# Six edits to the order, buffers and engines of a tuned two-block kernel on one core: group products given their own priority, a norm's short chain on GpSimd, a new pool for a residual

## Chip, cores and metric

One core of a Trainium2 chip. The metric is the device time of one execution in microseconds (us), the median of several runs; lower is better. Engines are written as in the profile: PE (TensorE matmuls), PEld (its weight loads), DVE (VectorE), ACT (ScalarE), POOL (GpSimd), SP (SyncE, which here only issues loads).

## The reference, cut to what matters

Two blocks in a row on 512 positions of width 1024, all in float32. The first mixes 8 heads of causal attention with 4 heads of a gated recurrence, adds a cross attention over 256 memory rows and a squared-ReLU feed-forward. The second holds a conv branch, a state-space branch (SSD) and a gated feed-forward. The lines the change touches:

```
x1  = x + concat([fox, rec]) @ w_out                  # output product of the mixer
kv  = rmsnorm(mem) @ w_xkv                            # memory keys, the very first product
x2  = rmsnorm(x1 + cross(x1) + ff(...), final_norm_g) # end of block one
hn  = rmsnorm(x2, mix_pre_g)                          # start of block two, right behind it
# SSD, 8 groups of 4 heads, chunks of 64 in the reference (128 in the kernel):
cb     = einsum("bclgn,bcsgn->bgcls", c_mat, b_mat)
y_diag = einsum("bgcls,bgrcls,bcsgrp->bclgrp", cb, decay_in, xdt)
y_off  = einsum("bclgn,bcgrpn,bgrcl->bclgrp", c_mat, prev, exp(a_cs))
y      = y_diag + y_off + x * d_skip
```

## The kernel before

Activations lie transposed, channels on the partitions and the 512 positions along the free axis, in 8 tiles of 128x512. A float32 product is made of three passes of a faster format: a value is split into a high part (`wh`, `xh`, cast on ACT) and a remainder (`wl`, `xl`, subtracted on DVE), and `mm3` (L148) adds hi·hi, hi·lo and lo·hi into one `acc` tile. `gemm_tile` (L154) makes one 128x512 tile of output from one 512 KB block of weights: 8 row blocks times 3 passes, 24 matmuls. Below, such a matmul (L150, L151 or L152) is called a product. The loads of weight blocks go through SP, their split through ACT (L138) and DVE (L139), and all 343 of these carry a priority of 300, so that they run ahead.

The engines' instruction lists are written by a scheduler from the program's order and from priorities. `tc.high_priority(n)` gives what stands inside it places counted from n ahead of where the program has it (a negative n: behind), and after the block the count goes on from where the block began; so a block and what follows it compete for the same places. `keep_in_program_order` pins an instruction to its place among others that are pinned. The scheduler decides the order once; on the chip each engine runs its list in that order, so whatever stands behind a waiting instruction waits too.

A norm over channels works thus: ACT squares each tile (L214), DVE adds the squares into `sqa` (L215), PE sums over partitions with a column of ones (`col_sum`, L223, 4 small matmuls), DVE scales (L229), POOL takes the power -0.5 (L231, `rsqrt_col`), PE spreads the result over the partitions (`row_bc`, L238, 4 matmuls) and ACT copies it out as a tile `R`.

Places the change touches, in the order of time:

- **The first blocks.** The memory keys, 8 blocks of 256-column products; block 0 is made by hand at L283, blocks 1 to 7 by `gemm_tile` at L291.
- **The output product** (L589). For each of 8 tiles the residual `xr` is loaded from `xT` into a tile of the pool `nrm` with the tag "sq", of which there are two. The squares of every norm use the same two.
- **The cross attention's** `nm` column (L637), 4 buffers of 8 bytes.
- **The end of block one** (L700 to L718). Two column sums are taken, of the squares (for `r1`) and of the squares times the gain (for `r2`). Both go through `rsqrt_col`, with three small DVE products between, and PE's L238 spreads `r2` as the tile `R`.
- **The SSD groups** (L983 on). For each g of 8, `group_a(g)` makes transposes (L861, L868), `cb` (L878), states (L886) and the products that give y (L916). Then `group_in(g+1)` makes four whole weight blocks with a short conv, then follow `glu`, `z_in`, gates and `group_b(g)`.

The matmuls of L916 are unlike the others. Each writes 64 output partitions (half r of two, by `r * 64`), so its weights are 128x64 and the profile gives its form as 128*64, where the products have 128*128. 14 of them make one half e of a group (8 with `mt` and `xd`, 6 with `Ct` and `st`): 2 x 8 x 14 = 224. In the trace each is two records, since its operands are plain float32. They are pinned to their order among themselves.

Of the kernel before, what the change touches and what calls it, by code (L numbers as in the profile page):

```python
# [6 lines left out]
F32 = mybir.dt.float32  # L7
# [4 lines left out]
ALU = mybir.AluOpType  # L12
# [22 lines left out]
LATE = 30  # L35
LATE2 = 15
LATE3 = 100
X0 = 0
X1 = 0
X2 = 30  # L40
X3 = 40
# [27 lines left out]
def _build(tc, nc, es, a, out):  # L69
# [79 lines left out]
    def mm3(ps, lh, ll, rh, rl, start, stop):  # L149
        T.matmul(out=ps, lhsT=lh, rhs=rh, start=start, stop=False)  # L150
        T.matmul(out=ps, lhsT=lh, rhs=rl, start=False, stop=False)  # L151
        T.matmul(out=ps, lhsT=ll, rhs=rh, start=False, stop=stop)  # L152

    def gemm_tile(src_blocks, xs, n=S):  # L154

# [110 lines left out]
    with es_mx:  # L266
        ms_ = []
        ac = nrm.tile([P, S], F32, tag="sqa", name="sqa")
        raw = raw0
        hi = whip.tile([P, 8, P], F32R, tag="wh", name="wh")  # L270
        lo = wlop.tile([P, 8, P], F32R, tag="wl", name="wl")
        nc.sync.dma_start(out=vec[:, 8:], in_=a["vec"][:, 8:])
        with tc.high_priority(2000):
            for k in range(0, 8, 2):
                c = slice(k, k + 2)
                G.tensor_copy(out=hi[:, c, :], in_=raw[:, c, :])
                V.tensor_tensor(out=lo[:, c, :], in0=raw[:, c, :], in1=hi[:, c, :].bitcast(F32), op=ALU.subtract)
                for kk in (k, k + 1):
                    ms_.append(split_act(mt[kk], vcol("norm_mem_g", kk), pl=pmx, n=M, tag="m"))
        ps0 = acc.tile([P, S], F32, tag="acc", name="acc")  # L280
        for k in range(8):
            mm3(ps0[:, :M], hi[:, k, :], lo[:, k, :], *ms_[k], k == 0, k == 7)
            if k in (1, 3, 5):  # L283

                for _ in range(FILL):
                    tc.keep_in_program_order(T.matmul(out=wps[:, 0:P], lhsT=ones, rhs=ones, start=True, stop=True))
        for n in range(8):
            if n == 2:
                for k in range(8):
                    nc.sync.dma_start(out=h[k], in_=a["xT"][k * P:(k + 1) * P, :])  # L290
            ps = gemm_tile([(a["w_xk"][n], 8)], ms_, M) if n else ps0  # L291
            A.copy(out=mk[n // 2][:, n % 2, :], in_=ps[:, :M])
        with tc.high_priority(400):
            for k in range(8):
                sq_acc(ac[:, :M], k, mt[k])
        Rm = pm.tile([P, M], F32, tag="Rm", name="Rm", bufs=1)
        with tc.high_priority(400):
            rm = rsqrt_col(col_sum(ac, 2), 2, D)
        with tc.high_priority(-X3):
            A.copy(out=Rm, in_=row_bc(rm, 2))  # L300
        ax = nrm.tile([P, S], F32, tag="sqa", name="sqa")
        for k in range(8):
            sq_acc(ax, k, h[k])
        for n in range(8):
            V.tensor_tensor(out=mk[n // 2][:, n % 2, :], in0=mk[n // 2][:, n % 2, :], in1=Rm, op=ALU.mult)
        R, rc = norm_fin(ax, D, 4, pl=pmx, late=X3)
        xs = []
        for k in range(8):
            V.scalar_tensor_tensor(out=h[k], in0=h[k], scalar=vcol("norm_mix_g", k), in1=R, op0=ALU.mult, op1=ALU.mult)
            xs.append(split_act(h[k]))  # L310
        for hf in range(2):
            def cb(j, ps):
                for i in range(2):
                    A.activation(out=mv[2 * hf + i][:, j, :], in_=ps[:, i * M:(i + 1) * M], func=AF.Copy,
                                 scale=rm[:, j:j + 1])
            gemm_tok(a["w_xv"][hf], ms_, 2, cb)


    with ExitStack() as ea:
# [264 lines left out]
        for i in range(4):  # L584
            g_gg(i)
        eh.close()
        ys = [split_act(mix[k]) for k in (4, 5, 6, 7, 0, 1, 2, 3)]
        h = []
        for n in range(8):  # L589
            xr = nrm.tile([P, S], F32, tag="sq", name="xr")  # L590
            nc.scalar.dma_start(out=xr, in_=a["xT"][n * P:(n + 1) * P, :])
            ps = gemm_tile([(a["w_out"][n], 8)], ys)
            t = hres.tile([P, S], F32, tag=f"h{n}", name=f"h1_{n}")
            V.tensor_tensor(out=t, in0=xr, in1=ps, op=ALU.add)  # L594
            h.append(t)
# [11 lines left out]
    with ExitStack() as ec:  # L607
# [19 lines left out]
        def cross_head(hd, q):  # L627
            PTh = pc.tile([P, 2, S], F32R, tag="PTh", name="PTh", bufs=1)
            PTl = pc.tile([P, 2, S], F32R, tag="PTl", name="PTl", bufs=1)
            for j in range(4):  # L630
                sl = slice(j * P, (j + 1) * P)
                ps = mA()
                mkh, mkl = mks[hd]
                for kk in range(2):
                    qh, ql = q[kk]
                    mm3(ps[:, :M], qh[:, sl], ql[:, sl], mkh[:, kk, :], mkl[:, kk, :], kk == 0, kk == 1)
                nm = pc.tile([P, 2], F32, tag="nm", name="nm", bufs=4)  # L637
                V.tensor_reduce(out=nm[:, 0:1], in_=ps[:, :M], axis=AX.X, op=ALU.max, negate=True)
                Pm = pc.tile([P, M], F32, tag="Pm", name="Pm", bufs=3)
                A.activation(out=Pm, in_=ps[:, :M], func=AF.Exp, bias=nm[:, 0:1], accum_out=nm[:, 1:2])  # L640
                V.reciprocal(out=nm[:, 1:2], in_=nm[:, 1:2])
                V.tensor_scalar(out=Pm, in0=Pm, scalar1=nm[:, 1:2], scalar2=None, op0=ALU.mult)
                pt = mB()
                for i in range(2):
                    T.transpose(out=pt[:, i * P:(i + 1) * P], in_=Pm[:, i * P:(i + 1) * P], identity=ident)
                pt = pt[:, :M].rearrange("p (i c) -> p i c", c=P)
                A.copy(out=PTh[:, :, sl], in_=pt)
                V.tensor_tensor(out=PTl[:, :, sl], in0=pt, in1=PTh[:, :, sl].bitcast(F32), op=ALU.subtract)
# [58 lines left out]
        sq_acc(ac2, k, h[k], vcol("final_norm_g", k))  # L707
    r1 = ctile([P, 4], F32, "r1")
    with tc.high_priority(-LATE2):
        V.tensor_copy(out=r1, in_=rsqrt_col(col_sum(ac1, 4), 4, D))  # L710
        v2 = nrm.tile([P, 4], F32, tag="rv2", name="rv2", bufs=1)
        V.tensor_tensor(out=v2, in0=col_sum(ac2, 4), in1=r1, op=ALU.mult)
        V.tensor_tensor(out=v2, in0=v2, in1=r1, op=ALU.mult)
        r2 = rsqrt_col(v2, 4, D)
        V.tensor_tensor(out=r2, in0=r2, in1=r1, op=ALU.mult)
    R = pre.tile([P, S], F32, tag="R12", name="R12")
    with tc.high_priority(-2 * LATE2):
        A.copy(out=R, in_=row_bc(r2, 4))  # L718
# [211 lines left out]
    def group_b(g, ys, zs):  # L930
# [4 lines left out]
            sq_acc(ac, e, zs[e])  # L935
        with tc.high_priority(-APRI):
            r = rsqrt_col(col_sum(ac, 4, mC), 4, 256)
        with tc.high_priority(-BPRI):
            Rg = row_bc(r, 4, mC)
            res = []  # L940
            for e in range(2):
                V.scalar_tensor_tensor(out=zs[e], in0=zs[e], scalar=vcol("ssm_norm_g_2", 2 * g + e), in1=Rg, op0=ALU.mult,
                                       op1=ALU.mult)
                res.append(split_act(zs[e]))
# [36 lines left out]
    cur = group_in(0, early)  # L981
    gq = list(range(8, 16)) + list(range(8))
    for g in range(8):  # L983
        ys = group_a(g, *cur)
        bg(BG[1])
        if g < 7:
            cur = group_in(g + 1)
# [252 lines left out]
```

## Time and profile before

| what | value |
|---|---|
| median of 3 runs | 1916.11 us (1915.81 to 1916.19) |
| the profiled execution: its time, its span | 1916.54 us, 1914.8 us |
| mean granted clock of PE | 0.997 of full speed |
| busy share of the span: PE, PEld, DVE, ACT, POOL | 99%, 82%, 63%, 45%, 5% |

The span is the time from the first to the last instruction; 1.74 us of the execution lie around it. Matmuls overlap in the pipeline of PE, so a record of 0.39 us doesn't mean that products come 0.39 us apart. The time of a place on PE is read from the starts of neighbouring records, and that is how the numbers below are made. What stands in brackets behind a row is idle time of that engine just before, and what ended it.

### The profile page before, as it was taken

How to read it: one execution, taken by the hardware profiler on the slowest of the kernel's cores; microseconds unless marked ns; L12 is line 12 of the kernel's file. 1: busy time of each engine (PE TensorE's matmuls, PEld its weight loads, DVE VectorE, ACT ScalarE, POOL GpSimd, SP SyncE). 2: the span in 40 equal slices, each digit the busy share in tenths (PEclk: the TensorE clock that was granted, in tenths of full speed). 3: DMA queues.
4: the chain of work that ended last, by engine and by line, in shares of the span. 5: the costliest groups of instructions: out<-in, count | busy, mean ns of one | idle time of the engine just before them, and what ended most of it. 6: DMA issues, size and time to landing. Idle time of an engine off the chain costs nothing.

```text
span 1914.8 us, 25080 instructions
## 1 busy us (share of the span) xinstructions
PE 1892.4 (99%) x9680; PEld 1573.7 (82%) x9680; DVE 1207.1 (63%) x1886; ACT 861.7 (45%) x1393; POOL 101.8 (5%) x198
## 2 busy tenths in 40 slices
PE   9999999999999999999999999999999999999997
PEld 8887776877888888877888888888888988888897
DVE  6744756655443344467888989578997774324456
ACT  6524547444331233348545553545344653222344
POOL 1001110000000000011110110110000000000000
PEclk9999999999999999999999999999999999999999
DMA  7412212322323333344333333333345532233244
GB/s 259 132 57 86 67 54 80 100 66 78 94 95 98 99 99 104 110 95 142 119 122 108 108 119 105 107 115 103 102 141 186 165 91 98 83 116 98 90 130 145
DMA packets 67542, 208.84 MB, mean 109 GB/s; under 512 B 8536, under 2 KB 15448, under 8 KB 67424
## 3 DMA queue, kind: packets, MB, share of 16 engines
q1 hardware_dynamic: 57856, 184.09, 30.9%
q0 software_dynamic: 5968, 16.87, 3.0%
q10 hardware_dynamic: 3600, 6.30, 0.9%
q8 instruction: 76, 1.25, 0.3%
q14 instruction: 42, 0.34, 0.1%
HBM read 198.71 MB, written 8.54 MB: 108 GB/s over the span
## 4 chain that ended last, share of the span: by engine, by line
PE 51%; issue 2%; DVE 1%; DMA 1%; ACT 0%; POOL 0%; POOLq 0%; DVEq 0%; ACTq 0%
PE acc L150 16%; PE acc L151 16%; PE acc L152 16%; PE pb L916 1%; PE pa L886 1%; PE pc L238 0%; PE pa L878 0%; PE pa L868 0%; PE pc L223 0%; PE pa L238 0%; DMA ab<-acsd 0%; DMA wr<-w_dn 0%; PE pa L223 0%; POOL rc L231 0%; PE pa L861 0%
## 5 line engine op out<-in xcount | busy, mean ns | idle before, releaser
L138 ACT CAST wh<-wr 128x1024 fp32r<-128x1024 f32 (+1 forms) x343 | 347.1, 1013 | 714.7 <-PE acc L151 585.1
L139 DVE TENSOR_TENSOR wl<-wr,wh 128x1024 fp32r<-128x1024 f32 (+1 forms) x343 | 403.2, 1176 | 287.4 <-ACT wh L138 277.8
L150 PE MATMUL acc<-yh,wh 128*128 128x512 f32 (+1 forms) x1112 | 432.9, 390 | 0.1
L152 PE MATMUL acc<-yh,wl 128*128 128x512 f32 (+1 forms) x1112 | 431.2, 388 | 0.0
L151 PE MATMUL acc<-yl,wh 128*128 128x512 f32 (+1 forms) x1112 | 429.8, 387 | 0.0
L152 PE MATMUL acc<-xh,wl 128*128 128x512 f32 (+1 forms) x832 | 313.7, 377 | 0.3 <-DVE wl L139 0.3
L150 PE MATMUL acc<-xh,wh 128*128 128x512 f32 (+1 forms) x832 | 313.7, 378 | 0.3 <-DVE h L594 0.3
L151 PE MATMUL acc<-xl,wh 128*128 128x512 f32 (+1 forms) x832 | 313.1, 377 | 0.0
L150 PEld LDWEIGHTS acc<-yh,wh 128*128 128x128 f32 x1112 | 209.1, 188 | 42.0 <-issue 1.4
L152 PEld LDWEIGHTS acc<-yh,wl 128*128 128x128 f32 x1112 | 209.1, 188 | 40.9
L151 PEld LDWEIGHTS acc<-yl,wh 128*128 128x128 f32 x1112 | 209.1, 188 | 40.3 <-DVE yl L202 0.4
L150 PE MATMUL acc<-uh,wh 128*128 128x512 f32 (+1 forms) x520 | 183.9, 354 | 0.0
L151 PE MATMUL acc<-ul,wh 128*128 128x512 f32 (+1 forms) x520 | 183.7, 353 | 0.0
L152 PE MATMUL acc<-uh,wl 128*128 128x512 f32 (+1 forms) x520 | 183.6, 353 | 0.0
L807 DVE SCALAR_TENSOR_TENSOR cv<-gp,vec,cv 128x512 f32<-128x512 f32 x240 | 177.6, 748 | 6.0 <-ACT cv L805 3.0
L150 PEld LDWEIGHTS acc<-xh,wh 128*128 128x128 f32 x832 | 157.1, 189 | 29.3 <-issue 1.5
L152 PEld LDWEIGHTS acc<-xh,wl 128*128 128x128 f32 x832 | 157.2, 189 | 28.7 <-issue 1.8
L151 PEld LDWEIGHTS acc<-xl,wh 128*128 128x128 f32 x832 | 157.2, 189 | 27.0 <-issue 1.2
L152 PEld LDWEIGHTS acc<-uh,wl 128*128 128x128 f32 x520 | 98.3, 189 | 13.5
L150 PEld LDWEIGHTS acc<-uh,wh 128*128 128x128 f32 x520 | 98.3, 189 | 13.4
L151 PEld LDWEIGHTS acc<-ul,wh 128*128 128x128 f32 x520 | 98.4, 189 | 13.3
L231 POOL TENSOR_TENSOR rc<-rv,mhalf 128x4 f32<-128x4 f32 (+1 forms) x25 | 29.7, 1188 | 966.4 <-DVE rv L229 883.2
(364 smaller groups left out, 2111.8 us busy)
## 6 DMA issues: line engine op xcount, KB each, us to landing
wr<-w SPq DMA_DIRECT2D x64, 512.0 KB, 3.8
wr<-w_gu SPq DMA_DIRECT2D x44, 512.0 KB, 3.5
wr<-w_out SPq DMA_DIRECT2D x24, 512.0 KB, 3.5
wr<-w_dn SPq DMA_DIRECT2D x24, 512.0 KB, 3.6
wr<-w_xs SPq DMA_DIRECT2D x16, 512.0 KB, 3.5
wr<-w_glu SPq DMA_DIRECT2D x16, 512.0 KB, 3.5
ab<-acsd POOLq DMA_DIRECT2D x32, 256.0 KB, 3.6
wr<-w_z SPq DMA_DIRECT2D x16, 512.0 KB, 3.5
```

What stands on the lines that cost most here:

```text
L138: A.copy(out=hi[:, :n], in_=raw[:, :n])
L139: V.tensor_tensor(out=lo[:, :n], in0=raw[:, :n], in1=hi[:, :n].bitcast(F32), op=ALU.subtract)
L150: T.matmul(out=ps, lhsT=lh, rhs=rh, start=start, stop=False)
L151: T.matmul(out=ps, lhsT=lh, rhs=rl, start=False, stop=False)
L152: T.matmul(out=ps, lhsT=ll, rhs=rh, start=False, stop=stop)
L231: G.tensor_tensor(out=r[:, :nt], in0=v[:, :nt], in1=mhalf[:, :nt], op=ALU.pow)
L807: yield V.scalar_tensor_tensor(out=o, in0=gp[:, t:t + S], scalar=cw(t), in1=o, op0=ALU.mult, op1=ALU.add)
L886: T.matmul(out=ps[:, 0:256], lhsT=Bt[:, c, :], rhs=xw[:, c].rearrange("p r d -> p (r d)"), start=True, stop=True)
L916: m = T.matmul(out=dst[r * 64:r * 64 + 64, c * P:(c + 1) * P], lhsT=lh, rhs=rh, start=True, stop=True)
```

## The change

1. Block 0 of the memory keys is made by pairs of row blocks, with hi·mh, lo·mh and hi·ml for each pair. Block 1 is made by a new function `gemm_lo_last`: all 16 products with `wh`, then the 8 with `wl`.
2. `xr` has a pool of its own, `pxr`, with two buffers.
3. `nm` has 8 buffers instead of 4, which moves the rest of its pool from an offset of 32 bytes to one of 64.
4. At the end of block one `v1` and `v2` are scaled on DVE, and the rest of the chain for `r1` and `r2` (two powers, three products, one addition on 128x4) is on POOL.
5. `group_a` stands in `tc.high_priority(-40)` for group 0 and in `tc.high_priority(0)` for groups 1 to 7. For group 7 the spread of the norm in `group_b` is set 24 further back.
6. `X0` goes from 0 to 10; it is the offset of one norm in the tail.

```diff
+G0 = 40
-X0 = 0
+X0 = 10
+    def gemm_lo_last(src, xs, n):
+        ps = acc.tile([P, S], F32, tag="acc", name="acc")
+        wh, wl = wblock(src, 8)
+        for w, e in ((wh, 0), (wh, 1), (wl, 0)):
+            for k in range(8):
+                T.matmul(out=ps[:, :n], lhsT=w[:, k, :], rhs=xs[k][e], start=w is wh and e + k == 0, stop=w is wl and k == 7)
+        return ps
...
-        for k in range(8):
-            mm3(ps0[:, :M], hi[:, k, :], lo[:, k, :], *ms_[k], k == 0, k == 7)
-            if k in (1, 3, 5):
+        for k in range(0, 8, 2):
+            for i, (w, e) in enumerate(((hi, 0), (lo, 0), (hi, 1))):
+                for kk in (k, k + 1):
+                    T.matmul(out=ps0[:, :M], lhsT=w[:, kk, :], rhs=ms_[kk][e], start=i + kk == 0, stop=i + kk == 9)
+            if k < 6:
...
-            ps = gemm_tile([(a["w_xk"][n], 8)], ms_, M) if n else ps0
+            ps = ps0 if n == 0 else gemm_lo_last(a["w_xk"][n], ms_, M) if n == 1 else gemm_tile([(a["w_xk"][n], 8)], ms_, M)
...
+        pxr = ea.enter_context(pool("pxr", 2, reuse_waits="tile"))
-            xr = nrm.tile([P, S], F32, tag="sq", name="xr")
+            xr = pxr.tile([P, S], F32, tag="xr", name="xr")
...
-                nm = pc.tile([P, 2], F32, tag="nm", name="nm", bufs=4)
+                nm = pc.tile([P, 2], F32, tag="nm", name="nm", bufs=8)
...
-        V.tensor_copy(out=r1, in_=rsqrt_col(col_sum(ac1, 4), 4, D))
+        v1 = nrm.tile([P, 4], F32, tag="rv", name="v1")
+        V.tensor_scalar(out=v1, in0=col_sum(ac1, 4), scalar1=1.0 / D, scalar2=EPS, op0=ALU.mult, op1=ALU.add)
-        V.tensor_tensor(out=v2, in0=col_sum(ac2, 4), in1=r1, op=ALU.mult)
-        V.tensor_tensor(out=v2, in0=v2, in1=r1, op=ALU.mult)
-        r2 = rsqrt_col(v2, 4, D)
-        V.tensor_tensor(out=r2, in0=r2, in1=r1, op=ALU.mult)
+        V.tensor_scalar(out=v2, in0=col_sum(ac2, 4), scalar1=1.0 / D, scalar2=None, op0=ALU.mult)
+        G.tensor_tensor(out=r1, in0=v1, in1=mhalf, op=ALU.pow)
+        G.tensor_tensor(out=v2, in0=v2, in1=r1, op=ALU.mult)
+        G.tensor_tensor(out=v2, in0=v2, in1=r1, op=ALU.mult)
+        G.tensor_scalar(out=v2, in0=v2, scalar1=EPS, scalar2=None, op0=ALU.add)
+        r2 = nrm.tile([P, 4], F32, tag="rc", name="r2", bufs=4)
+        G.tensor_tensor(out=r2, in0=v2, in1=mhalf, op=ALU.pow)
+        G.tensor_tensor(out=r2, in0=r2, in1=r1, op=ALU.mult)
...
-        with tc.high_priority(-BPRI):
+        with tc.high_priority(-BPRI if g < 7 else -BPRI - 24):
...
-        ys = group_a(g, *cur)
+        with tc.high_priority(-G0 if g == 0 else 0):
+            ys = group_a(g, *cur)
```

What this does to the instruction lists is shown at three places. The first is PE's list in group 1, first half. L916 is the line of the column-tiled matmuls, L936 after the change; L150 to L152 (L151 to L153 after) are the products of the weight block that is running. Before:

```order
L150 MATMUL acc<-yh,wh 128x512
L151 MATMUL acc<-yl,wh 128x512
L152 MATMUL acc<-yh,wl 128x512
L916 MATMUL pb<-mt,xd 64x128 [waits DVE_49]
L916 MATMUL pb<-mt,xd 64x128 x7
L916 MATMUL pb<-Ct,st 64x128 x2
L916 MATMUL pb<-Ct,st 64x128 [waits DVE_49]
```

And now:

```order
L153 MATMUL acc<-yh,wl 128x512
L936 MATMUL pb<-mt,xd 64x128 [waits DVE_49]
L151 MATMUL acc<-yh,wh 128x512
L936 MATMUL pb<-mt,xd 64x128
L152 MATMUL acc<-yl,wh 128x512
L936 MATMUL pb<-mt,xd 64x128
L153 MATMUL acc<-yh,wl 128x512
L936 MATMUL pb<-mt,xd 64x128
```

The 14 stood in one piece between two products; now one product stands between each two of them. Over all groups the 224 stood in 17 pieces (15 of 14, one of 12, one of 2) and now stand in 111: 8 of 14, two of 5, one of 2 and 100 single ones. The second half of a group stays in one piece in groups 0 to 6.

The second place is ACT's list ahead of the first group, from the second half of the first score tile `ab` to the SiLU of `Bt` (L785 before, L805 after), which PE's first transpose of the group (L861 before, L881 after) reads. Before:

```order
L905 ACTIVATE ab<-ab,acc__6612 128x128 [waits DMASW4_49]
L906 ACTIVATE mt<-ab 128x512 [waits Activation_49]
L785 ACT_TABLE_LOAD
L785 ACTIVATE xt<-xt 128x512 [waits DVE_49]
L138 CAST wh<-wr 128x1024 [waits DMAHW5_49,PE_49]
L785 ACTIVATE xt<-xt 128x512 [waits DVE_49]
L905 ACTIVATE ab<-ab,acc__6612 128x128
L785 ACTIVATE Bt<-Bt 128x512 [waits DVE_49]
```

And now:

```order
L139 CAST wh<-wr 128x1024 [waits DMAHW4_49,PE_49]
L805 ACT_TABLE_LOAD
L805 ACTIVATE xt<-xt 128x512 [waits DVE_49] x2
L798 COPY xp<-acc 128x512 [waits PE_49]
L801 ACTIVATE xt<-acc,vec 128x512 [waits DMASW1_49,DMASW0_49]
L925 ACTIVATE ab<-ab,acc__6614 128x128
L925 ACTIVATE ab<-ab,acc__6614 128x128 [waits DMASW4_49]
L926 ACT_TABLE_LOAD
L926 ACTIVATE mt<-ab 128x512 [waits Activation_49]
L139 CAST wh<-wr 128x1024 [waits DMAHW5_49,PE_49]
L805 ACT_TABLE_LOAD
L805 ACTIVATE Bt<-Bt 128x512 [waits DVE_49]
```

Ahead of `Bt` stand two more loads of a function table, one more cast of weights (the one with DMAHW4 stood ahead of all of this before), one more copy `xp` and one more activation of `xt`. PE's first transpose that reads it stands 7 products later than before.

The third place is PE's list at the norm behind the output product; L223 (L233) sums the squares, L238 (L248) spreads the result. Before:

```order
L223 MATMUL pc<-ones,sqa 128x1 [waits DVE_49]
L223 MATMUL pc<-ones,sqa 128x1 x3
L150 MATMUL acc<-xh,wh 128x512
L151 MATMUL acc<-xl,wh 128x512
L238 MATMUL pc<-ident,rc 128x128 [waits Pool_49]
L238 MATMUL pc<-ident,rc 128x128 x3
```

And now:

```order
L233 MATMUL pc<-ones,sqa 128x1 [waits DVE_49]
L233 MATMUL pc<-ones,sqa 128x1 x3
L151 MATMUL acc<-xh,wh 128x512
L152 MATMUL acc<-xl,wh 128x512
...
L152 MATMUL acc<-xl,wh 128x512
L248 MATMUL pc<-ident,rc 128x128 [waits Pool_49]
L153 MATMUL acc<-xh,wl 128x512
L248 MATMUL pc<-ident,rc 128x128
```

Two products stood between the sum and the spread, now 17, and the sum stands some 20 products further ahead.

Two more places, in words. At the end of block one 13 products stood between the second column sum (L223) and the spread of `r2` (L238); now 4 do. In the part of the tail that `X0` sets, the lists of all engines are the same as before.

## Rows read from the trace of the kernel before

**Rows 1.** The page, busy time, share of the span and count by engine.

```profile
PE 1892.4 (99%) x9680; PEld 1573.7 (82%) x9680; DVE 1207.1 (63%) x1886; ACT 861.7 (45%) x1393; POOL 101.8 (5%) x198
```

**Rows 2.** Timeline of PE, group 1, first half: start, us, line, form, count.

```profile
930.17 0.40 PE L152 MATMUL acc<-yh,wl 128*128 128x512 f32 x1
930.50 1.09 PE L916 MATMUL pb<-mt,xd 128*64 128x128 f32 x16
931.42 0.83 PE L916 MATMUL pb<-Ct,st 128*64 128x128 f32 x12
932.18 0.50 PE L150 MATMUL acc<-yh,wh 128*128 128x512 f32 x1
932.51 0.39 PE L151 MATMUL acc<-yl,wh 128*128 128x512 f32 x1
```

**Rows 3.** Timeline of PE, group 0, where two matmuls of L916 stand alone.

```profile
883.23 0.39 PE L150 MATMUL acc<-yh,wh 128*128 128x512 f32 x1
883.55 0.44 PE L916 MATMUL pb<-Ct,st 128*64 128x128 f32 x4
883.92 0.50 PE L151 MATMUL acc<-yl,wh 128*128 128x512 f32 x1
884.25 0.39 PE L152 MATMUL acc<-yh,wl 128*128 128x512 f32 x1
884.49 0.39 PE L150 MATMUL acc<-yh,wh 128*128 128x512 f32 x1
```

**Rows 4.** A tenth of that stretch, L916 alone: records under way.

```profile
core 0: us, PE busy (x) PEld busy (x), PEclk, DMA share, GB/s
883.50:883.60 0.10, 0.05 (x2) 0.05 (x2) 1.00 0.00 0
```

**Rows 5.** Timeline of PE, first block, where matmuls of another small form alternate with products.

```profile
80.55 0.50 PE L150 MATMUL acc<-xh,wh 128*128 128x512 f32 x1
80.99 0.22 PE L347 MATMUL pc<-ident,Fr 8*128 8x8 f32 x1
81.14 0.50 PE L151 MATMUL acc<-xl,wh 128*128 128x512 f32 x1
```

**Rows 6.** Timeline of PE, ahead of group 0.

```profile
872.41 0.39 PE L151 MATMUL acc<-yl,wh 128*128 128x512 f32 x1
874.25 0.55 PE L861 MATMUL pa<-ident,Bt 128*128 128x128 f32 x3 [1.45 <-ACT Bt L785]
```

**Rows 7.** Timeline of ACT, ahead of group 0.

```profile
869.99 1.28 ACT L785 ACT_TABLE_LOAD   x1
...
871.82 1.03 ACT L138 CAST wh<-wr 128x1024 fp32r<-128x1024 f32 x1
...
873.58 0.61 ACT L785 ACTIVATE Bt<-Bt 128x512 f32<-128x512 f32 x1
```

**Rows 8.** Timeline of PE, the first blocks.

```profile
12.95 0.39 PE L152 MATMUL acc<-mh,wl 128*128 128x256 f32 x1 [0.90 <-DVE wl L139]
...
18.09 0.61 PE L223 MATMUL pa<-ones,sqa 128*128 128x1 f32 x4 [0.20 <-DVE sqa L215]
```

**Rows 9.** Timeline of DVE, the same stretch.

```profile
17.09 0.95 DVE L215 TENSOR_TENSOR sqa<-sqa,sq 128x256 f32<-128x256 f32 x2
```

**Rows 10.** Timeline of PE, end of block one.

```profile
836.62 1.13 PE L238 MATMUL pa<-ident,rc 128*128 128x128 f32 x8 [0.88 <-DVE rc L715]
```

**Rows 11.** Timeline of POOL, the second power there.

```profile
835.27 1.01 POOL L231 TENSOR_TENSOR rc<-rv,mhalf 128x4 f32<-128x4 f32 x1 [2.56 <-DVE rv L229]
```

**Rows 12.** Groups of POOL by line and form: count, busy us, mean ns of one.

```profile
L508 POOL TENSOR_TENSOR nD<-nF,cmask 128x128 f32<-128x128 f32 x32 | 15.6, 491 | 76.0 <-DVE Sx L513 71.2 <-DMA nF<-nFd 3.6 <-DVE nm L518 1.0
...
L777 POOL MEMSET xp<- 128x3 f32 x28 | 2.8, 105 | 211.5 <-DMA gated<-gt 132.5 <-DVE xt L784 61.5 <-DVE gp L798 17.4
```

**Rows 13.** Timeline of PE, the norm behind the output product.

```profile
365.27 1.05 PE L223 MATMUL pc<-ones,sqa 128*128 128x1 f32 x8 [0.31 <-DVE sqa L215]
...
367.68 1.87 PE L238 MATMUL pc<-ident,rc 128*128 128x128 f32 x8 [0.78 <-POOL rc L231]
```

**Rows 14.** The stretch behind it: busy by engine (count), granted clock.

```profile
369.00:371.20 2.20, 2.20 (x8) 1.81 (x8) 1.13 (x1) 0.58 (x1) 0.00 (x0) 0.50 0.00 0
```

## The prediction

> **What bounds the kernel now.** The first look goes to the page's busy time: PE is at work for 1892.4 of 1914.8 us, and no other engine comes near [rows 1]. So PE's list sets the end almost everywhere. An edit gains only where PE stands idle or takes long for something, and costs wherever it makes PE's own list slower. The second look is the timeline of PE, read by the starts of records. A product comes 0.23 us behind the one before (884.25 to 884.49) [rows 3]. Whatever exceeds 0.23 per product is an idle stretch or the price of what stands between. The third look is at the places where PE idles, by the releaser in the brackets. The waits that the change aims at are small: 0.90 and 0.20 in the first blocks [rows 8], 0.31 and 0.78 behind the output product [rows 13], 0.88 at the end of block one [rows 10] and 1.45 ahead of group 0 [rows 6]. That is 4.5 us in all.
>
> The rows that decide are others: what PE loses where it goes from a product on the whole array to a matmul on part of it, and back.
>
> **The priority of the groups.** In groups 1 to 7 the matmuls of L916 now alternate with products. Their price is read from the trace.
>
> A run of 14: from 930.17, the last product ahead, to 932.51, the second behind, are 2.34 us [rows 2]. Two products account for 0.46, so the run costs 1.88.
>
> A run of two: from 883.23 to 884.25 are 1.02 us [rows 3]; less 0.46 this is 0.56.
>
> Twelve more matmuls cost 1.32, which is 0.11 each or 0.22 a pair. So of a run's price 0.34 is paid once, for going in and out, whatever its length.
>
> A single L916 isn't in the trace. Bounds: a matmul of 8 columns that alternates with products has a period of 81.14 − 80.55 = 0.59, so it costs 0.36 [rows 5]. It does far less work, so that is the floor. The ceiling is the pair, 0.56. Which is nearer depends on whether the two of a pair run beside one another, in the two halves of the array. In the first tenth of a microsecond of the lone pair two records are under way [rows 4], and the four records of the pair follow from 883.55 on, with 883.92 the next product [rows 3]. Two that start together means that a single one saves nothing by being alone: it leaves half of the array empty for as long as the pair would fill it. I take 0.56. If they ran one behind the other, it would be 0.56 − 0.11 = 0.45.
>
> Before: 15 runs x 1.88 + 0.34 + 6 x 0.22 for the run of 12 + 0.56 = 30.4. After: 8 x 1.88 + 100 x 0.56 + 0.56 + two runs of 5 at about 1.0 = 73.6. The term is **+43.2**; with singles at 0.45 +32, at 0.36 +23. Other matmuls of a group also stand alone between products now, but their form is 128*128, the products' own, and they pay no such price.
>
> The Trainium skill, TensorEngine Tiling (Array Packing), section Tiling Modes, says that a change of the tiling mode drains the engine, while a change of the tile alone doesn't; by that rule each of the 100 singles drains PE on its way in and out, and it speaks against this edit. The same section says that different tiles can work in parallel; by this the two of a pair run side by side and the term is +43.2, and without it +32. Rows 4 agree with it; the page gives no figure for a drain.
>
> **Group 0, 40 back.** PE's first transpose waited 1.45 for `Bt` [rows 6]. It now stands 7 products later, 7 x 0.23 = 1.6, which would just cover the wait. But ACT's list is changed too. Ahead of the SiLU of `Bt` at 873.58 come two more table loads at 1.28 and a cast at 1.03 [rows 7], 3.6 in all, and two further steps. ACT idles for some of that time before, so not all of it counts. Bounds: −1.5 (`Bt` not late) to +3.1 (all late: the steps make about 4.6 of delay against 1.6 of later need). I take +1.3.
>
> **The short chain on POOL.** PE's spread of `r2` waited 0.88 and started at 836.62 [rows 10], so PE was there at 835.74. It now stands 9 products earlier, at 833.7. The chain after the second column sum is now, on POOL, two products, an addition, a power and a product. POOL's power takes 1.01 [rows 11]. A four-column product or addition on POOL isn't in the trace. From below the memset of 3 columns bounds it, 0.105, and from above the product of 128 columns, 0.491 [rows 12]. The second sum is complete about four products ahead of the spread, 832.8, and one DVE step follows, so POOL starts near 833.0. The result comes at 833.0 + 1.01 + 4 x (0.105 to 0.491), 834.4 to 836.0. PE then idles 0.7 to 2.3 instead of 0.88: −0.2 to +1.4, and I take **+0.6**. The edit shortens the chain and gives the time back, since the list asks for the result earlier.
>
> **The pool for x.** The norm's squares no longer share buffers with `xr`, so they can be made as the tiles come. The sum stands 20 products further ahead and 17 products (3.9 us) instead of 2 separate it from the spread, which needs DVE's scale, POOL's 1.0 and little more. Both waits go, 0.31 + 0.78 [rows 13]. The stretch behind them ran for 2.2 us [rows 14] at a granted 0.50, the lower of its two levels (1.2 of 2.4 GHz), right after PE had idled twice: 8 records of work that would take half of that at full clock, so 1.1. Together −2.2; with the fall on the way down **−2.4** (bounds 0, if DVE's squares come late at the new place, and −3.0).
>
> **lo products last.** Block 1's wait for `wl` of 0.90 [rows 8] goes, since the 16 products with `wh` cover it. But the column sum of the squares, 0.20 late before, stands at the same place in PE's list and needs the squares on DVE that end at 18.04 [rows 9]. Nothing on PE is ahead of those: a load, a cast and DVE set them. So PE arrives earlier and waits there: **0** (bounds −1.2 and +0.5).
>
> **The rest.** `X0` changes no list: 0. `nm` shifts addresses alone: 0, and no row suggests otherwise. The 24 for group 7 moves a spread for which nothing waited: 0 (±0.5).
>
> **The sum.** 1916.54 + 43.2 + 1.3 + 0.6 − 2.4 = 1959.2 for the profiled execution. That lies 0.43 above the median of the runs, so the forecast is **1958.8**, 2.2% slower. A difference of 0.2%, 3.8 us, is about what a measurement of this kernel can tell from none.
>
> **Rivals.**
>
> *The price of a single is lower.* Part of going in and out may hide under a product, which rows 5 allow down to 0.36: 1916.1 + 23 − 0.5 = 1938.6; at 0.45 it is 1947.6. For it speaks that these are real alternations, where the run of two isn't one. Against it: an 8-column matmul leaves PE sooner than one of 128 columns with two records.
>
> *The time goes up further.* The 14 matmuls of a half need `mt` from DVE and `st`. Standing between products, a late one stops the products behind it, seven times. An idle stretch of 1 us each and the clock at half for 2 us behind each, as at 369 [rows 14], would be 7 x 2 = 14: 1973. Nothing shows that the operands are late there, and slower PE gives them more time.
>
> *The other side: PE loses nothing by alternating.* If a single one cost only its share of a run, 0.11, the term would be 15.0 + 11 + 0.6 + 2.0 − 30.4 = −2, and the waits would count: −2.4 behind the output product, −1.5 at group 0, −0.2 for the short chain and −1.2 in the first blocks at their best. That gives 1909. It decides below a price of 0.13 a single with my other terms, or 0.18 with these. Rows 5 show 0.36 for a matmul with far less work, so this needs the column-tiled form to be a cheaper guest than that one.
>
> *The change doesn't do what it says.* The order shows that the waits in the first blocks and at `r2` only move and that `X0` is without effect. This is in the sum already; without the first term it would be 1915.6, no change.
>
> **How the numbers follow.** Forecast, singles at 0.5 to 0.6 (1952 to 1966): 0.62. Cheaper singles (1936 to 1952): 0.20. Further loss (above 1966): 0.10. Alternating free: 0.05 faster, and 0.03 for no change. The range takes in the forecast and most of the cheaper singles: 1940 to 1967, about 0.82. Faster by over 0.2%: 0.05; within: 0.03; slower: 0.92.
>
> **What the changed profile would show.** The term of the groups: PE's timeline in groups 1 to 7 alternates L936 and products with a period near 0.79 and not 0.34, and PE's busy share stays near 99%. Group 0: idle ahead of L881 of over 1.45, ended by ACT. The short chain: L248 at `r2` idle 1 to 2, ended by POOL. The pool: no idle at L233 and L248 behind the output product and clock 1.00 there. First blocks: no idle at the `wl` product, over 1 us at L233. The prediction is wrong if the period in the groups is under 0.5, or if PE shows idle stretches of over a microsecond in each of them.

## The result: 2.9% slower

The changed kernel takes 1972.14 us (median of 4 runs, 1970.76 to 1973.87), the kernel before 1916.15 in the same comparison. The ratio is 1.0291, 95% interval 1.0274 to 1.0309. The forecast was 1958.8 and the range ended at 1967: the direction and the main term were right, the rest of the sum too small by 13 us.

The profile of the changed kernel has a span of 1969.0 us; lines are one to twenty higher than before (L150 is L151, L238 is L248, L916 is L936). The page's busy times answer to [rows 1]:

```profile
PE 1941.8 (99%) x9680; PEld 1585.5 (81%) x9680; DVE 1208.4 (61%) x1882; ACT 899.3 (46%) x1423; POOL 107.4 (5%) x202
```

PE has as many instructions as before and is busy for 49 us more. ACT has 38 us and 30 instructions more; by the traces these 30 are loads of function tables (73 instead of 43), 1.28 us each [rows 7]. Where the time went is read from the starts of the same product in both traces (the n-th of the 7856 that write an `acc` tile). This is worked out from the two traces, not a view of the profile:

```
product   starts before   starts now   now - before   what lies between it and the row above
    830       263.38         263.07        -0.31       first blocks, lo products last
    850       273.16         274.44        +1.27       a norm that the change doesn't touch
   1140       359.14         360.71        +1.58
   1300       422.00         420.67        -1.33       norm behind the output product, pool for xr
   3050       828.91         826.60        -2.31       cross attention, feed-forward
   3090       841.90         844.03        +2.12       spread of r2, chain on POOL
   3210       871.73         873.60        +1.87
   3330       908.42         913.11        +4.69       group 0
   5400      1449.53        1503.93       +54.40       groups 1 to 7
   7800      1895.17        1949.21       +54.04       tail
```

So nearly 50 us are lost in groups 1 to 7, 4.4 at the end of block one and 2.8 in group 0; 1.6 are lost where nothing was changed, 2.9 are gained behind the output product and 1.0 in the cross attention. This is one execution of each kernel; the experiments show which of these amounts hold in others.

**Groups 1 to 7.** The timeline of PE in group 1, first half, answers to [rows 2]:

```profile
938.05 0.39 PE L153 MATMUL acc<-yh,wl 128*128 128x512 f32 x1
938.37 0.43 PE L936 MATMUL pb<-mt,xd 128*64 128x128 f32 x2
938.73 0.49 PE L151 MATMUL acc<-yh,wh 128*128 128x512 f32 x1
939.16 0.43 PE L936 MATMUL pb<-mt,xd 128*64 128x128 f32 x2
939.52 0.49 PE L152 MATMUL acc<-yl,wh 128*128 128x512 f32 x1
```

From product to product, 938.73 to 939.52, are 0.79. Less 0.23 that is 0.56 for a single matmul of L936, the forecast's value to the hundredth. The period is 0.79 or 0.80 at 92 of the 100 and 0.68 at 8. Of the 0.79, 0.43 pass from the product's start to that of the narrow matmul and 0.36 from there to the next product. No idle time is shown: PE counts as busy all the while.

In group 7 there is a wait that the forecast didn't have. The timeline of PE there:

```profile
1416.69 0.39 PE L153 MATMUL acc<-yh,wl 128*128 128x512 f32 x1
1419.94 0.69 PE L151 MATMUL acc<-yh,wh 128*128 128x512 f32 x1 [2.86 <-ACT zs L870]
1420.43 0.63 PE L152 MATMUL acc<-yl,wh 128*128 128x512 f32 x1
1420.86 0.63 PE L153 MATMUL acc<-yh,wl 128*128 128x512 f32 x1
```

A product can't start because its PSUM tile is still to be read by the SiLU of `zs` (L870). The products behind come 0.43 apart instead of 0.23: the granted clock is 0.54 from 1419.9 to 1421.9. The timeline of ACT shows why the SiLU is late:

```profile
1415.02 0.62 ACT L211 CAST xh<-zs 128x512 fp32r<-128x512 f32 x1 [3.40 <-DVE zs L962]
1416.34 0.62 ACT L211 CAST xh<-zs 128x512 fp32r<-128x512 f32 x1 [0.70 <-DVE zs L962]
1416.93 1.04 ACT L139 CAST wh<-wr 128x1024 fp32r<-128x1024 f32 x1
1418.00 1.28 ACT L870 ACT_TABLE_LOAD   x1
1419.29 0.60 ACT L870 ACTIVATE zs<-acc 128x512 f32<-128x512 f32 x1
```

ACT idled for 3.40 us until DVE had scaled the group before (L962), with the SiLU queued behind that group's casts in ACT's list.

**The end of block one** answers to [rows 10, 11]. The timeline of PE, then that of POOL:

```profile
831.00 0.40 PE L153 MATMUL acc<-xh,wl 128*128 128x512 f32 x1
833.82 2.08 PE L248 MATMUL pa<-ident,r 128*128 128x128 f32 x8 [2.42 <-POOL r L735]
835.55 0.77 PE L151 MATMUL acc<-xh,wh 128*128 128x512 f32 x1
```

```profile
830.71 1.06 POOL L730 TENSOR_TENSOR rv<-rv,r 128x4 f32<-128x4 f32 x1 [0.30 <-DVE rv L727]
831.84 0.20 POOL L731 TENSOR_TENSOR rv<-rv,r 128x4 f32<-128x4 f32 x1
832.13 0.23 POOL L732 TENSOR_SCALAR rv<-rv 128x4 f32<-128x4 f32 x1
832.45 1.04 POOL L734 TENSOR_TENSOR r<-rv,mhalf 128x4 f32<-128x4 f32 x1
833.57 0.20 POOL L735 TENSOR_TENSOR r<-r,r 128x4 f32<-128x4 f32 x1
```

PE stands ready at 831.4 and gets its operand at 833.8. Of the four small operations three took 0.20 to 0.23 and one, the first product, 1.06. The windows of PE behind the wait (busy and count, granted clock, DMA) show the larger part of the loss:

```profile
833.80:839.20 5.40, 5.38 (x17) 0.50 0.11 46
839.20:842.00 2.80, 2.80 (x13) 0.89 0.00 0
```

For 5.4 us PE works at 0.50, its level of 1.2 GHz instead of 2.4, right after the idle stretch. The wait is 1.5 longer than the 0.88 of before; the rest of the 4.4, 2.9, is the clock. But that is this execution: four experiments below have the same chain and the same wait of 2.4 at this place (the first, third, fifth and ninth), and there it loses 3.2, 1.6, 3.0 and 1.6 in all. In the two with 1.6 the granted clock of the 22 us around it is 1.00, in this one 0.84.

**Group 0** answers to [rows 6, 7]; the timelines of PE and of ACT:

```profile
879.39 0.55 PE L881 MATMUL pa<-ident,Bt 128*128 128x128 f32 x3 [3.13 <-ACT Bt L805]
```

```profile
874.53 1.28 ACT L926 ACT_TABLE_LOAD   x1
875.83 0.63 ACT L926 ACTIVATE mt<-ab 128x512 f32<-128x512 f32 x1
876.36 1.03 ACT L139 CAST wh<-wr 128x1024 fp32r<-128x1024 f32 x1
877.41 1.28 ACT L805 ACT_TABLE_LOAD   x1
878.70 0.63 ACT L805 ACTIVATE Bt<-Bt 128x512 f32<-128x512 f32 x1
```

The SiLU of `Bt` starts 5.1 us later than in [rows 7] and PE needs it 3.5 later (the wait begins at 876.3 instead of 872.8); the two table loads and the cast stand ahead of it. The wait is 1.7 longer than before; the rest of the 2.8 goes with the clock, 0.91 from 872 to 892 where it was 1.00.

### The profile page after: what moved, and what is told of

It is laid out like the page before. It is cut to its first block, busy times and chain, and to the rows that moved or that the text cites. A ratio compares the mean times of both kernels' runs of the same rounds, so it can differ in the third digit from the quotient of the medians.

```text
span 1969.0 us, 25107 instructions
## 1 busy us (share of the span) xinstructions
PE 1941.8 (99%) x9680; PEld 1585.5 (81%) x9680; DVE 1208.4 (61%) x1882; ACT 899.3 (46%) x1423; POOL 107.4 (5%) x202
## 4 chain that ended last, share of the span: by engine, by line
PE 91%; issue 3%; DVE 2%; ACT 2%; DMA 1%; POOL 0%; SPq 0%; POOLq 0%; DVEq 0%; ACTq 0%
PE acc L151 27%; PE acc L152 26%; PE acc L153 26%; PE pb L936 3%; PE pa L477 1%; PE pb L563 1%; PE pc L248 1%; PE pa L906 1%; DVE wl L140 1%; ACT wh L139 0%; PE pc L233 0%; PE pa L248 0%; PE pb L535 0%; DMA ab<-acsd 0%; PE pb L575 0%
## 5 line engine op out<-in xcount | busy, mean ns | idle before, releaser
L151 PE MATMUL acc<-yh,wh 128*128 128x512 f32 (+1 forms) x1112 | 440.7, 397 | 2.9 <-ACT zs L870 2.9
L153 PE MATMUL acc<-yh,wl 128*128 128x512 f32 (+1 forms) x1112 | 437.8, 394 | 0.0
L152 PE MATMUL acc<-yl,wh 128*128 128x512 f32 (+1 forms) x1112 | 437.5, 394 | 0.0
L151 PE MATMUL acc<-xh,wh 128*128 128x512 f32 (+1 forms) x832 | 314.9, 380 | 0.7 <-DVE so L980 0.4
L153 PE MATMUL acc<-xh,wl 128*128 128x512 f32 (+1 forms) x832 | 314.7, 378 | 0.3 <-DVE wl L140 0.3
L152 PE MATMUL acc<-xl,wh 128*128 128x512 f32 (+1 forms) x832 | 314.6, 378 | 0.0
L151 PEld LDWEIGHTS acc<-yh,wh 128*128 128x128 f32 x1112 | 209.5, 188 | 49.8 <-issue 7.5
L152 PEld LDWEIGHTS acc<-yl,wh 128*128 128x128 f32 x1112 | 209.6, 188 | 45.6 <-issue 6.2
L153 PEld LDWEIGHTS acc<-yh,wl 128*128 128x128 f32 x1112 | 209.5, 188 | 44.5 <-issue 5.2
L151 PE MATMUL acc<-uh,wh 128*128 128x512 f32 (+1 forms) x520 | 183.9, 354 | 0.0
L152 PE MATMUL acc<-ul,wh 128*128 128x512 f32 (+1 forms) x520 | 183.7, 353 | 0.0
L153 PE MATMUL acc<-uh,wl 128*128 128x512 f32 (+1 forms) x520 | 183.6, 353 | 0.0
L151 PEld LDWEIGHTS acc<-xh,wh 128*128 128x128 f32 x832 | 157.7, 190 | 30.3 <-issue 1.7
L153 PEld LDWEIGHTS acc<-xh,wl 128*128 128x128 f32 x832 | 157.7, 190 | 28.7 <-issue 1.8
L152 PEld LDWEIGHTS acc<-xl,wh 128*128 128x128 f32 x832 | 157.9, 190 | 27.4 <-issue 1.2
L151 PEld LDWEIGHTS acc<-uh,wh 128*128 128x128 f32 x520 | 98.4, 189 | 13.5
L153 PEld LDWEIGHTS acc<-uh,wl 128*128 128x128 f32 x520 | 98.4, 189 | 13.4
L152 PEld LDWEIGHTS acc<-ul,wh 128*128 128x128 f32 x520 | 98.4, 189 | 13.4
```

## The experiments

Theory A, after the result: the 100 single matmuls cost 43 us, and the rest are idle stretches that other edits make on PE, each with a stretch at half clock behind it. Theory B: alternating costs less, and other moves of the order more. Theory C: a small matmul between large ones is dear whatever its form. "Before" is the time of the kernel before, taken on the same chip together with the experiment.

**Groups 1 to 7 back.**

```diff
-        with tc.high_priority(-G0 if g == 0 else 0):
-            ys = group_a(g, *cur)
+        if g == 0:
+            with tc.high_priority(-G0):
+                ys = group_a(g, *cur)
+        else:
+            ys = group_a(g, *cur)
```

> The changed kernel with the groups 1 to 7 at their old priority (their 14 matmuls stand in one piece again); all else as changed. Theory A (the 100 single column-tiled matmuls at 0.56 us cost 43 us, the rest of the 56 is idle stretches that the other edits make, each with PE at half clock behind it): 1972 - 43 = 1929, or 1924 if the 2.9 us wait for zs in group 7 and its half clock go too. Theory B (alternating costs about half of that, and the rest of the loss is from the chain on POOL, group 0 and the clock): 1940 to 1950.

Measured 1922.3, before 1917.6, ratio 1.0026 (1.0016 to 1.0035). The loss falls from 2.9% to 0.26% with this one line, some 50 us; the wait for `zs` is gone too. A, if a little more than it said.

**That edit alone, in the kernel before.**

```diff
+        if g > 0:
+            with tc.high_priority(0):
+                ys = group_a(g, *cur)
+        else:
+            ys = group_a(g, *cur)
```

> The kernel before with one edit, groups 1 to 7 of group_a under a priority of 0. Theory A: 1916 + 43 = 1959, up to 1964 if the wait for zs in group 7 comes with it. Theory B: 1937 to 1945.

Measured 1964.0, before 1917.6, ratio 1.0235 (1.0220 to 1.0251). The waits of PE, sums, times and longest:

```profile
PE acc L150 <- ACT zs L850: 2.9, 1, 2.9
```

The wait for `zs` belongs to this edit. 43 for the singles and 2.9 make 46, and 46.4 were measured: A. This kernel has 24 of the 30 further table loads (67).

**The same places, another form of the array.** `xd` gets a column block of zeros between its two halves, so that a matmul has weights of 128 columns and both halves add up in PSUM; the two with the same `Ct` become one. `y` of the first half takes over the buffer of `xw`, for space.

```diff
-            run = [(psd, c, xd[:, c, 2 * e + r, :], mts[r][:, c, :], r) ...
+            run = [(psd, c, xd[:, c, e, r:r + 2, :], mts[r][:, c, :], r == 1, r == 0) ...
-            run += [(pso_, c, st[:, c - 1, e * P + r * 64:e * P + r * 64 + 64], ...
+            run += [(pso_, c, st[:, c - 1, e * P:(e + 1) * P], C[:, c * P:(c + 1) * P], True, True) ...
```

> The changed kernel with the same interleaved order, but the matmuls of a group use the whole array: the two halves' weights are padded with zeros to 128 columns and added up in PSUM, and the two with the same Ct are one (11 matmuls of 128x128 per half instead of 14 of 128x64). Theory A (the price is that of changing the form of the array): 176 matmuls at 0.11 are 19 us where 72 were, so 1972 - 52 = 1920, within 5. Theory C (the price is that of a small matmul between large ones, whatever its form): 176 instead of 224 pieces, 1955 to 1965.

Measured 1937.6, before 1917.6, ratio 1.0097 (1.0081 to 1.0112): between the theories. The timeline of PE in group 1:

```profile
941.25 0.38 PE L936 MATMUL pb<-mt,xd 128*128 128x128 f32 x2
941.38 0.48 PE L151 MATMUL acc<-yh,wh 128*128 128x512 f32 x1
941.70 0.38 PE L936 MATMUL pb<-mt,xd 128*128 128x128 f32 x2
941.84 0.47 PE L152 MATMUL acc<-yl,wh 128*128 128x512 f32 x1
```

The period is 0.46, so a single one costs 0.23 and not the 0.11 that the expectation put in: it is two records, and 0.11 is the price of one. With 0.22 the 176 cost 39, and 1972 − 72 + 39 = 1939. 139 of the 176 stand alone. Alternating with products, the wide form costs 0.23 and the narrow one 0.56; a narrow one inside a piece costs 0.11. So it is going from one form to the other and back that is dear, and C falls. What the engine does in these 0.34 us no run shows.

**The two halves of a piece one after the other,** in the kernel before.

```diff
-... for c in range(4) for r in (1, 0)]
+... for r in (1, 0) for c in range(4)]
-... for c in range(1, 4) for r in (1, 0)]
+... for r in (1, 0) for c in range(1, 4)]
```

> The kernel before with the 14 of a run in another order: first those of one half of the array, then those of the other, so that neighbours mostly don't lie in different halves. In 8 halves the scheduler also splits the run in 10 and 4. If the two of a pair run side by side, each now takes 0.22 alone: 14 x 0.22 + 0.34 = 3.4 instead of 1.88, so +1.5 x 16 = +24 and 8 x 0.34 = 3 for the split runs, less what still pairs where the half changes: 1937 to 1943. If they run one behind the other: +3 at most, 1916 to 1920.

Measured 1929.6, before 1917.6, ratio 1.0055 (1.0040 to 1.0070): half of what was expected. The windows of L916 alone, 0.5 us each, in one such piece (the counts are records under way on PE and PEld):

```profile
888.20:888.70 0.50, 0.50 (x6) 0.50 (x7) 1.00 0.48 164
889.20:889.70 0.50, 0.50 (x13) 0.50 (x12) 1.00 0.22 77
```

At first, with one half's matmuls alone, half as many records are under way as later, when those of the other half come in beside them. So two of different halves do run side by side, and a lone one does leave half of the array empty. The size was wrong because the second half's matmuls start well before the first half is through: in this piece 0.5 us after the first of them, at 888.70 against 888.20.

**The chain on POOL alone,** in the kernel before (the diff of the change, edit 4).

> The kernel before with one edit, the short chain of the norm at the end of block one on POOL. Theory A (the order asks for the result 9 products earlier, but the chain on POOL is as long as the old one): PE idles 2.4 us ahead of the spread instead of 0.88, +1.5; with PE at half clock behind it, as in the changed kernel, 3 us more: 1917.6 to 1921. Rival (the chain on one engine is shorter and PE gets its result sooner): 1915 to 1916.

Measured 1925.3, before 1915.85, ratio 1.0048 (1.0031 to 1.0065): worse than either theory. The waits of PE:

```profile
PE pa L867 <- ACT Bt L791: 3.7, 1, 3.7
...
PE pa L238 <- POOL r L721: 2.4, 1, 2.4
```

At the spread it loses 3.0 against the kernel before, within what was expected. A further 4.4 go in group 0, which the edit doesn't name: ACT's list has two more table loads ahead of `Bt` here too. So those that the forecast put down to edit 5 come with edit 4. Why the scheduler puts them there isn't shown; they also stand there when the spread comes later (the experiment before last).

**Group 0 alone, 40 back,** in the kernel before.

```diff
+        if g == 0:
+            with tc.high_priority(-40):
+                ys = group_a(g, *cur)
+        else:
+            ys = group_a(g, *cur)
```

> The kernel before with one edit, group 0 of group_a 40 back. Here the order has no further table load ahead of the SiLU of Bt, but two copies of xp and two activations of xt, 2.7 us, and PE's first transpose stands 5 products (1.1 us) later. Theory A (what stands ahead of Bt on ACT sets the wait): the wait stays at 1.4 to 3 us, 1916 to 1919. Rival (the edit does what its 40 seem meant for): the wait of 1.45 goes, 1914.5.

Measured 1915.9, before 1915.85, ratio 0.9996 (0.9987 to 1.0006). In the trace the wait for `Bt` is 0.60 instead of 1.45. That is 0.85 gained, between the two expectations, and too little for the times to tell. No further table load stands ahead of `Bt`; six more stand elsewhere (49).

**The pool for xr alone.**

```diff
+        pxr = ea.enter_context(pool("pxr", 2, reuse_waits="tile"))
-            xr = nrm.tile([P, S], F32, tag="sq", name="xr")
+            xr = pxr.tile([P, S], F32, tag="xr", name="xr")
```

> The kernel before with one edit, the pool of its own for xr. Both waits behind the output product and the stretch at half clock go: -2.4 to -3.9, 1912 to 1914. Rival: the squares come late at the new place as well, 1915 to 1916.

Measured 1915.4, before 1915.85, ratio 0.9992 (0.9983 to 1.0001). That is the rival's number, though not its mechanism: PE has no idle time at either place. In the trace they gain 2.8, but two other stretches at half clock fall into this execution, at 268 and at 872. The median gained 0.5, and the interval takes in no change. A good part of the 2.8 isn't the pool's. PE's windows over these places, in the kernel before and in the kernel with the groups' edit alone, whose list is the same here:

```profile
365.00:380.00 15.00, 13.95 (x75) 0.89 0.17 57
```

```profile
365.00:380.00 15.00, 13.91 (x81) 1.00 0.17 59
```

Of the seven kernels with the old pool, the clock falls behind the two waits in two, the kernel before and the one with the lo products last. In the other five it is 1.00, and the same products come 1.4 us earlier than in the kernel before, without any edit here. So the pool removes some 1.4 us in most executions, and 2.8 where the clock would have fallen.

**The lo products last alone** (edit 1 of the change).

> The kernel before with one edit, the products with the low parts last in the first two blocks of the memory keys. The wait for wl goes and the column sum of the squares waits in its place: 0 to -0.5 for the whole kernel, so no change that can be measured, and in the trace no idle time ahead of a product with wl in block 1 and over 0.5 us ahead of the column sum. Rival: both go, -1.2.

Measured 1918.1, before 1915.85, ratio 1.0009 (1.0000 to 1.0019). The timeline of PE shows the wait in its new place, where [rows 8] had 0.20:

```profile
18.51 0.61 PE L232 MATMUL pa<-ones,sqa 128*128 128x1 f32 x4 [1.46 <-DVE sqa L224]
```

No gain, as expected. In this execution the clock from 18 to 24 is 0.72, and the trace loses 1.9 in the first blocks, where that of the changed kernel gained 0.3.

**The pieces together, all else as changed.**

```diff
-            for i, (dst, c, lh, rh, r) in enumerate(run):
-                m = T.matmul(...)
+            with tc.high_priority(60):
+                for i, (dst, c, lh, rh, r) in enumerate(run):
+                    m = T.matmul(...)
```

> The changed kernel with one addition: the 14 matmuls of a half stand under a priority of 60 ahead inside group_a. By the order they stand in one piece again (15 of 14, one of 12, one of 2), while all other instructions of the groups keep the places that the change gave them. Theory A (the price is that of the 100 single column-tiled matmuls): 1972 - 43 = 1929, within 5. Theory B (the other moves of the groups cost a good part of it): over 1940.

Measured 1923.8, before 1918.0, ratio 1.0037 (1.0021 to 1.0053). The waits for `zs` (2.4) and `Bt` (4.9) are there still, and 48 us of the 56 are gone. The time lies 5 us below A's 1929, so what went is the 43 and some more; B is out. Of the other matmuls on PE nearly all (9206 of 9232) keep their order, so this is the place of the 14. The lists of the other engines do change: ACT has 63 table loads here and 73 in the changed kernel.

**Neither the groups nor the chain:** the changed kernel with the diff of the first experiment, and the old lines in place of edit 4.

> The changed kernel without the priority of groups 1 to 7 and without the chain on POOL; the lo products last, the pool for xr, nm, group 0, group 7 and X0 stay. Theory A (those two edits hold all of the loss): 1912 to 1916. Theory B (the others lose too): 1918 or more.

Measured 1914.2, before 1918.0, ratio 0.9982 (0.9973 to 0.9991). Theory A, and the other edits together gain 0.18%. Of all versions this has the lowest ratio to the kernel before.

**The chain on POOL, its spread later.**

```diff
-    with tc.high_priority(-2 * LATE2):
+    with tc.high_priority(-2 * LATE2 - 28):
         A.copy(out=R, in_=row_bc(r2, 4))
```

> The kernel before with the chain on POOL and the spread of r2 28 places later, so that 18 products instead of 4 stand between the second column sum and the spread. Theory A (the loss at r2 is where the order asks, not how long the chain is): no idle time ahead of the spread. But ACT's order ahead of Bt still has the two further table loads, and a wait of 3 to 4 us stays there: 1916 to 1919 instead of 1925. Rival (R comes too late for the early tiles): idle time moves to the first products behind, 1920 or more.

Measured 1924.8, before 1918.0, ratio 1.0035 (1.0021 to 1.0049). The rival. The waits of PE:

```profile
PE pa L867 <- ACT Bt L791: 3.6, 1, 3.6
...
PE pc L765 <- ACT dtc L766: 1.6, 1, 1.6
```

The wait at the spread is gone, and one of 1.65 stands at the transposes of the step sizes (L765, L759 before), which need `R`; it was 0.19 before.

**The pool, group 0 and a later spread,** in the kernel before: the diffs of these three experiments together, the chain as it was.

> The kernel before with the pool for xr, group 0 set 40 back, and the spread of r2 28 places later with its chain as before. By the order the SiLU of Bt stands ahead of the score tiles on ACT. The waits at 365, 367, 836 and 872 go, 3.4 us, and the stretch at half clock with them where there was one: 1911 to 1914. Rival: R comes later and the early tiles of the second block wait for it, 1916 or more.

Measured 1917.6, before 1918.0, ratio 0.9999 (0.9991 to 1.0008). The rival again. The waits of PE:

```profile
PE pb L918 <- DVE mt L909: 3.2, 1, 3.2
...
PE pc L761 <- ACT dtc L762: 1.6, 1, 1.6
```

All four waits at which it was aimed are gone, and 4.9 us stand at two others. By the program both lie on the path from `R` to the first group; no run takes them apart.

## Why the prediction was off

- **The groups: right.** The term was 43.2. The period of 0.79, the order and the two experiments that move the 14 matmuls alone bear it out (46 with the wait that came along, 48). By the starts of the products in both traces, the column-tiled matmuls of groups 1 to 7 cost 43.3 more than before. Choosing the pair's price over that of an 8-column matmul was right, for the reason given: two halves run side by side.
- **The step that failed first is what else that edit moves.** "Nothing shows that the operands are late there" looked only at L916's own operands. The edit also moved ACT's list, and the SiLU of `zs` came behind a cast that waits for DVE: 2.86 and, in this execution, 1.8 at half clock; with the edit alone the same wait had a clock of 1.00 behind it. The forecast had 0 for it, and its rival of further loss looked for it at another place.
- **The chain on POOL was mis-sized:** +0.6 forecast, +4.4 measured at the spread. The idle stretch was 2.42 where 0.7 to 2.3 had been given, so the bounds on the small operations nearly held, though one of them took 1.06. Missing was the price of the clock behind an idle stretch, 2.9 here and 0.1 to 1.7 in four others with the same wait. [Rows 14] showed it, and the forecast used it only where such a stretch goes away.
- **Group 0:** +1.3 forecast, +2.8 measured, inside the bounds of −1.5 and +3.1; the cause was right on ACT, but it comes with the chain on POOL and not with the 40. That the size came near is in part luck: with the chain on POOL the same place lost 3.2, 4.4 and 5.3 in the first, fifth and ninth experiment.
- **The pool:** −2.4 forecast, −2.9 measured, with no idle time and a clock of 1.00. The waits went for the reason given. But half of the term, the stretch at half clock of [rows 14], was luck of one execution of the kernel before; in five of seven it isn't there, and the edit alone gained 0.5 in the median.
- **lo products last:** 0 forecast, −0.3 in the trace, and the wait moved to the column sum as said: 0.52 in the changed kernel, 1.46 with the edit alone.
- **`nm`:** put at 0 because no row suggested otherwise; it gains 1.0, see the last section.
- **No step named** the 1.6 us at 268; see there too.

Of the 13 us, by this one execution, 3.8 are the chain, 1.5 group 0, 4.7 the wait for `zs` and 1.6 the clock at 268; the pool and the first blocks take 0.8 back. Some 2.5 are left. 1.8 of them lie between profiled executions and medians (1.4 for the changed kernel, whose profiled execution took 1970.76, and 0.4 that the forecast took off for the kernel before). Of the rest, `nm` takes 1.0 back, groups 1 to 7 lose another 1.8, of which 0.4 is a wait for `so` in group 7, and what else they lose stays open.

## What to carry to other kernels

Matmuls that use part of the array belong together: here a piece of 14 costs 1.9 us and 14 single ones 7.8, with no idle time to point to it. When a scheduler makes the list, even a priority of 0 can break such a piece up, so look at the list, and at the lists of the other engines that the edit moves, ahead of pricing any wait. And a wait that is removed from one place of a chain can come back at the next, as long as the chain itself isn't shorter: so it was with the lo products and with both later spreads. A stretch at half clock seen in one profile may not be there in the next, so its price doesn't belong in full into a forecast.

## What the runs showed of the hardware that was not expected

- The same idle stretch may or may not cost the clock. At 268 all fourteen kernels have the same list and the same 0.83 to 0.84 us of waiting for a power on POOL. The windows of PE from 266 to 274 (granted clock behind the count) show 1.00 in six of them and less in eight. The kernel before and the changed one:

```profile
266.00:274.00 8.00, 7.16 (x43) 1.00 0.20 67
```

```profile
266.00:274.00 8.00, 7.16 (x33) 0.79 0.21 69
```

  Where it falls, it costs 1.5 to 1.6 us. Executions of the kernel before differ by up to 6.2 us on one chip (1914.92 to 1921.12), more than most edits of this change are worth. That such places make up this spread is likely, but not shown, since each kernel has one profile.
- On POOL two of the three products of 128x4 in the chain took 0.20 and the first of them 1.06. The last one also came right behind a power, so that isn't the reason; the reason stays open.
- Edit 3 gains 1.0 us, though it changes no list and no wait there. The output product of the cross attention (`w_xo`) consists of 192 products. In an unbroken stretch of them they come 0.232 to 0.233 us apart in the nine kernels without the edit of `nm` and 0.227 in the five with it, without idle time. PE's windows over most of them, before and now (the count of records, then the granted clock):

```profile
437.00:475.00 38.00, 38.00 (x165) 1.00 0.29 86
```

```profile
437.00:475.00 38.00, 38.00 (x169) 1.00 0.28 97
```

  These products don't read `nm`; what the edit does to them is that the addresses behind it in its pool move, from an offset of 32 bytes to one of 64. The lo products, the pool for `xr`, the chain and both priorities of the groups were each run without it and leave the time between these products as it was. `nm` alone was not run, so addresses are the likely cause and not a shown one.
